# Two PSUM banks per GLA tile instead of four: values, keys and scores in one, output and state update in the other

## The chip, the cores and the metric

The kernel runs on one core of a Trainium2 chip. The metric is the time of one execution on the device, in microseconds (us); the median of three runs of the kernel before is 1786.33 us. All data is 32-bit floating point.

Engines: PE is the matrix engine, ACT the scalar engine, DVE the vector engine, POOL the general-purpose engine, and SP the engine that issues most transfers. PE writes its results to PSUM, of which this kernel uses eight banks of 512 fp32 numbers per partition; ACT and DVE read them from there.

## The reference

One decoder layer is computed for 2048 new tokens of one prompt and for 8 short continuations of 8 tokens each. The input x is projected by one wide matrix; the pieces feed sliding-window attention and a gated linear attention (GLA), both are gated, projected, merged, projected again, and a layer norm ends it. The change is in GLA, whose reference is a scan over chunks, with one state S per head:

```
b = jnp.cumsum(gc, axis=1); b_last = b[:, -1]
qt = qc * jnp.exp(b); kt = kc * jnp.exp(-b); kend = kc * jnp.exp(b_last[:, None] - b)
o_inter = jnp.einsum('bthk,bhkv->bthv', qt, S)
A = jnp.where(causal, jnp.einsum('bthk,bshk->bhts', qt, kt), 0.0)
o_intra = jnp.einsum('bhts,bshv->bthv', A, vc)
S = jnp.exp(b_last)[..., None] * S + jnp.einsum('bshk,bshv->bhkv', kend, vc)
```

There are 4 heads, keys of 128 and values of 256 numbers per head. The output o_inter + o_intra is divided by its root mean square and multiplied by a gate.

## The kernel before

**The projections** fill nearly all of PE's time. A product of fp32 numbers is made of three products of a reduced type: an operand is split into a high and a low part (`split`, lines 141 to 145: ACT casts the high part, line 142, then DVE or POOL subtracts it, line 143), and high x high, high x low and low x high are added up (lines 1335 to 1337). Large projections save one product in eight by a scheme with seven sums of blocks. There are four accumulator banks, pd0 to pd3, used in turn; ACT or DVE reads each out in `combine` and in the sinks (lines 199 to 229 and 384 to 410). The work is done in passes: x0, x1, x2 (input projections of three token ranges), then a0, u0, a1, u1, a2, u2 (the projections after attention and after GLA). Operands of a pass are loaded into tiles r (from xT, ua_d or ug_d) and split into tiles x.

**The side work.** Attention and GLA run as small pieces between the groups of the projections. Each piece has a due time in ticks of the projections' progress (`at`, `tick`, lines 124 to 130); `gla_phase` (line 1190) sets the times. PE's instructions stand in exactly the written order (`manual_schedule`, line 66). For the other engines the order is sorted when the kernel is built, by a scheduler that reckons with the waits between instructions; each engine then takes its own list strictly in order.

**GLA per tile of 128 tokens and head.** 64 such tiles are worked, in three phases; in the last phase each head ends with the continuations' tokens (`samp_a`, `samp_b`).

- `gla_v` (line 1071): PE transposes the values (two, line 1076) and the decayed keys (one, line 1077) into one bank; ACT and DVE split the 384 columns into gv and gl.
- `gla_a` (line 1087): PE makes the scores (line 1090) in a second bank; DVE copies them under the causal mask (line 1092) and ACT and POOL split them into ah.
- `gla_b` (line 1107), some one and two thirds of a tile's time later: PE reads the old state (line 1119) into the output's bank op, makes the state's update with three products into a fourth bank sp, and adds the three products of scores and values to op (all by the helper `three`, line 1113). DVE makes the new state from sp (line 1127; 1125 for a head's first tile). ACT squares and sums op (line 1101), POOL takes the power (lines 1102 and 1103), ACT scales op into on (line 1104).
- `gla_c` (line 1132), again as much later: PE transposes on into another bank (line 1136), and DVE multiplies it by the gate sg (line 1138). `gla_store` sends the result to ug_d, from where the passes u0 to u2 load it.

**The banks.** All side work takes its PSUM tiles from one pool of four banks (line 64), by `pa()`:

```
psa = ctx.enter_context(tc.tile_pool(name="psa", bufs=4, space=PSUM))
```

A request gets a bank that an earlier request had, and the first product into it waits until that tile's last reader is done. Which bank a request gets is fixed when the kernel is built. In the program before, the transposes of line 1136 mostly follow the state update of a later tile's `gla_b` (its reader is line 1127), the state's update follows a tile of scores (reader: line 1092), the output follows an earlier output (reader: line 1104), the scores follow an earlier line 1136 (reader: line 1138), and the values follow earlier values (readers: lines 142 and 143). The low-rank gate projection (`lowrank`, line 544) and attention take their tiles from the same pool.

Of the kernel before, what the change touches and what calls it, by code (L numbers as in the profile page):

```python
# [21 lines left out]
P = 128  # L22
# [15 lines left out]
HK = 128  # L38
HV = 256
# [18 lines left out]
def kernel(ctx, tc, io):  # L58
    nc = tc.nc
    mm = nc.tensor.matmul  # L60
# [15 lines left out]
    def pa():  # L76
        return psa.tile([P, 512], F32, tag="pa", name="pa")
# [18 lines left out]
    def mt(tag, n, bufs, dt=F32, name=None):  # L96
        return M["p"].tile([P, n], dt, tag=tag, name=name or tag, bufs=bufs)
# [43 lines left out]
    def split(dst_h, dst_l, src, eng=nc.vector):  # L141
        pin["a"] = nc.scalar.copy(dst_h, src)  # L142
        i = eng.tensor_tensor(dst_l, src, dst_h.bitcast(F32), ALU.subtract)  # L143
        if eng is nc.vector:
            pin["d"] = i
# [111 lines left out]
    for n, (kind, s, kh, prs) in enumerate(sets):  # L257
        start_of.append(len(groups))
        base.append(int(tk))
        for pr_ in prs:  # L260
# [5 lines left out]
            elif seq[n] in PLAIN:  # L266
                jk = [(j, k) for j in range(2) for k in range(2)]
                for c in range(2):
                    for j, k in jk if kind == "a" else [(j, k) for k, j in jk]:
                        q, p = pr_[j]  # L270
# [730 lines left out]
    def rot(key):  # L1001
        r = R[key][cnt[key] % len(R[key])]
        cnt[key] += 1
        return r
# [66 lines left out]
    def gla_v(B, i):  # L1071
        n = P if i < B["nt"] else NS
        ts = slice(i * P, i * P + n)
        tp = pa()
        for m in range(2):
            nc.tensor.transpose(tp[:n, m * P:(m + 1) * P], B["zvv"][:, m, ts], ident)
        nc.tensor.transpose(tp[:n, HV:HV + HK], B["k2"][:, ts], ident)
        if n == P:
            B["gv", i] = rot("gv"), rot("gl")
            split(*B["gv", i], tp[:, :HV + HK])  # L1080
            return
        g = mt("pr2", 2 * GU, 6, name="gs")[:, :HV + HK]
        nc.scalar.copy(g[:n], tp[:n, :HV + HK])
        nc.vector.tensor_copy(g[NS:], tp[:n, :HV + HK])
        B["gv", i] = g[:, :HV], g[:, HV:]

    def gla_a(B, i):
        ts = slice(i * P, (i + 1) * P)
        ap = pa()
        mm(ap[:, :P], B["k"][:, ts], B["q"][:, ts], start=True, stop=True)  # L1090
        A_ = rot("a")
        nc.vector.copy_predicated(A_, cmask.bitcast(U32), ap[:, :P])
        x = rot("ah")
        split(x[:, :P], x[:, P:], A_, nc.gpsimd)
        B["a", i] = x[:, :P], x[:, P:]

    def gla_norm(B, key, o, n):

        on = rot("on")
        sq = small([P, 1], "sq")  # L1100
        nc.scalar.activation(on[:n], o, AF.Square, scale=1.0 / 16, accum_out=sq[:n])
        nc.gpsimd.tensor_scalar(sq[:n], sq[:n], EPS, None, op0=ALU.add)
        nc.gpsimd.tensor_tensor(sq[:n], sq[:n], mhalf[:n], ALU.pow)
        nc.scalar.mul(on[:n], o, sq[:n])
        B["on", key] = on

    def gla_b(B, i):
        ts = slice(i * P, (i + 1) * P)
        gh, gl = B["gv", i]

        def three(ps, w, x, start):
            for j, (a, c) in enumerate(((w[0], x[0]), (w[1], x[0]), (w[0], x[1]))):
                mm(ps, a, c, start=start and j == 0, stop=(j == 2))  # L1113

        gv, kT2 = (gh[:, :HV], gl[:, :HV]), (gh[:, HV:], gl[:, HV:])
        S = sstate.get(B["h"])
        op = pa()
        if S is not None:
            mm(op[:, :HV], B["qb"][:, ts], S_t[S], start=True, stop=False)  # L1119
        sp = pa()  # L1120
        three(sp[:, :HV], kT2, gv, True)
        three(op[:, :HV], B["a", i], gv, S is None)
        Sn = S_free.popleft()
        if S is None:
            nc.vector.tensor_copy(S_t[Sn], sp[:, :HV])
        else:
            nc.vector.scalar_tensor_tensor(S_t[Sn], S_t[S], B["e1"][:, i:i + 1], sp[:, :HV], ALU.mult, ALU.add)
            S_free.append(S)
        sstate[B["h"]] = Sn
        gla_norm(B, i, op[:, :HV], P)  # L1130
# [59 lines left out]
    def gla_phase(s, t0, st):  # L1190
# [5 lines left out]
        for h, (c0, T_) in ([(h, c) for c in GCH[s] for h in range(GH)] if s == 1 else  # L1196
                            [(h, c) for h in range(GH) for c in GCH[s]]):
            if True:
# [10 lines left out]
                for i in range(nt):  # L1209
                    at(tt(u + i), lambda B=B, i=i: gla_v(B, i))  # L1210
                    at(tt(u + i), lambda B=B, i=i: gla_a(B, i))
                    at(tt(u + i + 5 / 3), lambda B=B, i=i: gla_b(B, i))
                    at(tt(u + i + 10 / 3), lambda B=B, i=i: gla_c(B, i, P, i * P))
# [3 lines left out]
                if last:  # L1217
                    u += 1
                    at(o - 5, lambda B=B: samp_state(B))
                    at(o, lambda B=B: gla_v(B, B["nt"]))  # L1220
                    at(o + 2, lambda B=B: samp_a(B))
                    at(tt(u - 1 + 0.5) + 2, lambda B=B: nc.sync.dma_start(io["o_sp"][B["h"]], S_t[sstate[B["h"]]]))
                    o = max(o + 6, tt(u - 1 + 4 / 3) + 1)
                    at(o, lambda B=B: samp_b(B, 0))
                    at(o + 2, lambda B=B: samp_b(B, 2))
                    at(o + 5, lambda B=B: gla_c(B, "s", NS, B["Tp"]))
                    at(max(o + 6, tt(u + 4 / 3) + 1), lambda B=B: gla_store(B))
                else:
                    at(tt(u + 7 / 3) + 1, lambda B=B: gla_store(B))
        return int(b0 + st * (nu + 7 / 3) + 3)  # L1230

    for s in range(MS):
        for t in range(2):
            B = dict(s=s, t=t)
# [73 lines left out]
    for g, (n, q, i, s, p, b, ch) in enumerate(groups):  # L1308
# [19 lines left out]
        ps = (banks[b] if b < 4 else banks2[b - 4])[:, :T]  # L1328
        if n == U2 and g >= start_of[U2] + 16:
            ps = banks2[b][:, :T]  # L1330
        for k in range(q.kh):
            ks, ts = slice(k * P, (k + 1) * P), slice(k * T, (k + 1) * T)
# [261 lines left out]
```

## Time and profile before

| | |
|---|---|
| median of three runs, without the profile | 1786.33 us (1783.8 to 1787.14) |
| the profiled execution's own time | 1796.17 us |
| its span, first to last instruction | 1794.4 us |
| granted clock of PE, mean over the span | 0.992 |
| DMA | 452.36 MB, mean 252 GB/s |

The profile is of one execution. A row of its list of groups gives line, engine, operation, what is written <- what is read, the count, the busy time and the mean duration in ns, and behind the second bar the idle time of the engine ahead of these instructions, with what ended it. A row of the waits gives who waited <- for whom, the sum in us, the number of waits and the longest. A row of the timeline gives the start and the duration in us, and in square brackets the idle time ahead of it. A row of the table by stretches gives the stretch, its length, the busy time (and the count) of PE, PE's weight loads, DVE, ACT and POOL, then the granted clock of PE as a share of the full one, the DMA engines' share, and GB/s. Buffer numbers are left out of names: pa is any tile of the pool of four banks, pd any of the four accumulators.

### The profile page before, as it was taken

Reading aid. Unit: us, or ns where it says so; the run is one execution under the profiler, and the core shown is the slowest. Engines: PE = TensorE matmul, PEld = TensorE weight load, DVE = VectorE, ACT = ScalarE, POOL = GpSimd, SP = SyncE. Lnnn points to the kernel's source line nnn. Section 1 sums busy time; section 2 is a strip of 40 time slices with the busy share of each in tenths; the row PEclk is TensorE's granted clock in tenths of the full one; section 3 lists DMA queues with packets and bytes.
Section 4 is the critical chain, followed back from the end, with each engine's and each line's share of the span. In section 5 each row is a group of like instructions: output and inputs, shape, how many; then the busy total and the mean of one; then the engine's idle time right before and its main releaser. Section 6 shows DMA issues by size and latency. Waiting matters only on the chain.

```text
span 1794.4 us, 31950 instructions
## 1 busy us (share of the span) xinstructions
PE 1755.9 (98%) x11154; PEld 1653.1 (92%) x11154; DVE 1102.7 (61%) x2178; ACT 866.6 (48%) x2084; POOL 375.3 (21%) x522
## 2 busy tenths in 40 slices
PE   8999999998999999999999999999999999999998
PEld 8899988998999999999999999999989989998887
DVE  6655679778555477548655447645856645536666
ACT  4565566566574465557466346645433432311100
POOL 5334624454111000013211100000122122121111
PEclk9999999999999999999999999999999999999999
DMA  6789977986978977886879788879889968965531
GB/s 215 252 306 333 327 236 241 312 290 215 308 260 284 304 252 236 282 288 208 281 251 313 228 289 275 267 241 336 282 230 250 298 178 224 320 155 189 168 108 53
DMA packets 290913, 452.36 MB, mean 252 GB/s; under 512 B 29213, under 2 KB 210133, under 8 KB 290736
## 3 DMA queue, kind: packets, MB, share of 16 engines
q1 hardware_dynamic: 262896, 415.04, 70.3%
q10 hardware_dynamic: 20464, 26.24, 4.1%
q0 software_dynamic: 7392, 9.04, 3.6%
q8 instruction: 88, 1.44, 0.3%
q14 instruction: 73, 0.60, 0.1%
HBM read 297.52 MB, written 153.57 MB: 251 GB/s over the span
## 4 chain that ended last, share of the span: by engine, by line
PE 78%; DMA 8%; DVE 5%; ACT 4%; issue 2%; POOL 2%; SPq 1%; DVEq 0%; ACTq 0%; POOLq 0%
PE pd L1335 18%; PE pd L1337 18%; PE pd L1336 18%; PE pd L1399 3%; PE pd L1400 3%; PE pd L1398 3%; PE pa L1113 2%; PE pa L832 1%; PE pa L818 1%; PE pa L786 1%; PE pa L1119 1%; DMA ug_d<-sg 1%; POOL ws L348 1%; DMA mg_d<-fin 1%; PE pa L1335 1%
## 5 line engine op out<-in xcount | busy, mean ns | idle before, releaser
L143 DVE TENSOR_TENSOR wp<-ws,wp 128x512 fp32r<-128x512 f32 (+1 forms) x396 | 276.5, 701 | 204.9 <-ACT wp L142 189.4
L142 ACT CAST wp<-ws 128x512 fp32r<-128x512 f32 (+1 forms) x396 | 234.1, 595 | 193.9 <-PE pd L1337 129.8
L348 POOL TENSOR_TENSOR ws<-ws 128x256 f32<-128x256 f32 x162 | 148.4, 943 | 166.5 <-DVE wp L143 100.9
L143 POOL TENSOR_TENSOR ah<-aper,ah 128x128 fp32r<-128x128 f32 x64 | 36.2, 566 | 399.5 <-ACT ah L142 399.5
L1399 PE MATMUL pd<-woh,x 128*128 128x512 f32 (+1 forms) x272 | 102.4, 377 | 0.0
L1400 PE MATMUL pd<-wol,x 128*128 128x512 f32 (+1 forms) x272 | 102.4, 377 | 0.0
L1398 PE MATMUL pd<-woh,x 128*128 128x512 f32 (+1 forms) x272 | 102.4, 377 | 0.0
L384 ACT COPY m<-pd 128x352 f32<-128x352 f32 x146 | 66.3, 454 | 70.5 <-PE pd L1337 64.8
L1335 PE MATMUL pd<-x3h,wp 128*128 128x352 f32 x292 | 97.3, 333 | 1.8 <-DMA wp<-wk_w_g 1.2
L1335 PE MATMUL pd<-x6h,wp 128*128 128x352 f32 x292 | 97.0, 332 | 2.0 <-ACT m L384 2.0
L1335 PE MATMUL pd<-x1h,wp 128*128 128x352 f32 x292 | 96.7, 331 | 2.2 <-DVE fin L405 2.1
L1335 PE MATMUL pd<-x7h,wp 128*128 128x352 f32 x292 | 97.7, 334 | 0.9 <-DVE fin L201 0.9
L1335 PE MATMUL pd<-x5h,wp 128*128 128x352 f32 x292 | 96.6, 331 | 0.0
L1335 PE MATMUL pd<-x2h,wp 128*128 128x352 f32 x292 | 96.3, 330 | 0.0
L1335 PE MATMUL pd<-x4h,wp 128*128 128x352 f32 x292 | 96.2, 330 | 0.0
L1337 PE MATMUL pd<-x1h,wp 128*128 128x352 f32 x292 | 94.0, 322 | 0.7 <-DVE wp L143 0.7
L1337 PE MATMUL pd<-x7h,wp 128*128 128x352 f32 x292 | 94.6, 324 | 0.0
L1337 PE MATMUL pd<-x3h,wp 128*128 128x352 f32 x292 | 94.5, 324 | 0.0
L1336 PE MATMUL pd<-x7l,wp 128*128 128x352 f32 x292 | 94.4, 323 | 0.0
L1336 PE MATMUL pd<-x3l,wp 128*128 128x352 f32 x292 | 94.3, 323 | 0.0
L1337 PE MATMUL pd<-x6h,wp 128*128 128x352 f32 x292 | 94.2, 323 | 0.0
L1336 PE MATMUL pd<-x6l,wp 128*128 128x352 f32 x292 | 94.0, 322 | 0.0
(462 smaller groups left out, 5475.2 us busy)
## 6 DMA issues: line engine op xcount, KB each, us to landing
wp<-wk_w_g SPq DMA_DIRECT2D x96, 512.0 KB
ws<-w_g SPq DMA_DIRECT2D x120, 256.0 KB
wk_w_g<-wp SPq DMA_DIRECT2D x48, 512.0 KB
wp<-wk_w_ra SPq DMA_DIRECT2D x32, 512.0 KB
wp<-wk_w_rg SPq DMA_DIRECT2D x32, 512.0 KB
ws<-w_at SPq DMA_DIRECT2D x53, 256.0 KB
wp<-wk_w_at SPq DMA_DIRECT2D x24, 512.0 KB
ws<-w_pg SPq DMA_DIRECT2D x48, 256.0 KB
```

The costliest lines, as they stand in the source:

```text
L142: pin["a"] = nc.scalar.copy(dst_h, src)
L143: i = eng.tensor_tensor(dst_l, src, dst_h.bitcast(F32), ALU.subtract)
L348: nc.gpsimd.tensor_tensor(o[:, c], x[:, c], y[:, c], op)
L384: nc.scalar.copy(A[i], ps)
L786: mm(ps[kv][:, j, k0:], A["q"][x][r, g0 + j, :], A["k"][y][r, k0:], start=(n == 0), stop=(n == 2), tile_position=(kv * HD, 0))
L1113: mm(ps, a, c, start=start and j == 0, stop=(j == 2))
L1335: mm(ps, wh, xh[:, ts], start=first, stop=False, skip_group_check=ch)
L1336: mm(ps, wh, xl[:, ts], start=False, stop=False, skip_group_check=ch)
L1337: mm(ps, wl, xh[:, ts], start=False, stop=(k == q.kh - 1 and not (type(i) is tuple and i[1] == 0)), skip_group_check=ch)
L1398: mm(ps, xh[:, xs], hi, start=(k == 0), stop=False)
L1399: mm(ps, xl[:, xs], hi, start=False, stop=False)
L1400: mm(ps, xh[:, xs], lo, start=False, stop=(k == KT - 1))
```

## The change

`gla_v` asks for a bank as before and now makes the scores too, in the columns behind values and keys (256 + 128 + 128 = 512). `gla_a` asks for none and reads the scores there. `gla_b` asks for one bank, whose first half is the output and whose second half is the state's update; the update's three products come first, then the read of the old state, then the three products of scores and values. A tile asks the pool three times instead of five. The arithmetic is the same.

```diff
@@ gla_v
-        tp = pa()
+        tp = B["va", i] = pa()
...
         nc.tensor.transpose(tp[:n, HV:HV + HK], B["k2"][:, ts], ident)
         if n == P:
+            mm(tp[:, HV + HK:], B["k"][:, ts], B["q"][:, ts], start=True, stop=True)
             B["gv", i] = rot("gv"), rot("gl")
@@ gla_a
-        ap = pa()
-        mm(ap[:, :P], B["k"][:, ts], B["q"][:, ts], start=True, stop=True)
+        ap = B["va", i][:, HV + HK:]
@@ gla_b
-        op = pa()
+        ps = pa()
+        op, sp = ps[:, :HV], ps[:, HV:]
+        three(sp[:, :HV], kT2, gv, True)
         if S is not None:
             mm(op[:, :HV], B["qb"][:, ts], S_t[S], start=True, stop=False)
-        sp = pa()
-        three(sp[:, :HV], kT2, gv, True)
         three(op[:, :HV], B["a", i], gv, S is None)
```

Lines 1090 and 1119 of the kernel before are lines 1079 and 1121 of the changed one; the other lines named here keep their numbers from line 1092 on, except 1119 and 1120.

What this makes of the lists of the engines is shown at three places. The first is PE's list at a `gla_b` between two products of the projections; gv and gl are the split values and keys, gb the query operand, S the old state, ah the split scores.

```order
 L1336 MATMUL pd_75<-x1l,wp 128x352
 L1337 MATMUL pd_75<-x1h,wp 128x352
-L1119 MATMUL pa<-S_219,gb 128x256
 L1113 MATMUL pa<-gv 128x256
 L1113 MATMUL pa<-gv,gl 128x256
 L1113 MATMUL pa<-gl,gv 128x256
+L1121 MATMUL pa<-S_219,gb 128x256
 L1113 MATMUL pa<-gv,ah 128x256 x2
 L1113 MATMUL pa<-gl,ah 128x256
```

The read of the old state moved behind the three products of the state's update; nothing else moved, and this is so in every tile with an old state. Elsewhere on PE, only the line number of the scores differs, and PE's list of the projections is the same.

The second place is while pass a1 runs (its sink is line 219) and the operand x(0, 1) of a later pass is made. On ACT, before:

```order
L142 CAST x(0, 0)_17890<-r_17783 128x352 x2
L142 CAST wp<-ws 128x256 x2
L142 CAST gv<-pa 128x384
L1051 ACTIVATE em<-dm 128x256
L1052 ACTIVATE ek<-ek 128x256
L142 CAST ah<-aper_209 128x128
L1053 ACTIVATE dm<-dm 128x256
L1054 ACTIVATE gb<-gb 128x256
L142 CAST x(0, 1)_17949<-r_17812 128x352
L142 CAST wp<-ws 128x256
```

and in the changed kernel:

```order
L142 CAST x(0, 0)_17765<-r_17660 128x352
L142 CAST wp<-ws 128x256
L142 CAST x(0, 1)_17823<-r_17688 128x352
L142 CAST gv<-pa 128x384
L1051 ACTIVATE em<-dm 128x256
L1052 ACTIVATE ek<-ek 128x256
L1053 ACTIVATE dm<-dm 128x256
L1054 ACTIVATE gb<-gb 128x256
L142 CAST ah<-aper_209 128x128
L142 CAST wp<-ws 128x256
```

The cast of x(0, 1), which needs a loaded tile r, moved ahead of the split of the values and of the decay factors. On DVE at the same place, before:

```order
L143 TENSOR_TENSOR gl<-pa,gv 128x384
L143 TENSOR_TENSOR wp<-ws,wp 128x256
L219 SCALAR_TENSOR_TENSOR fin<-part,pd_77 128x352
L1056 COPY e_17167<-gb 128x2
L1067 TENSOR_TENSOR em<-zkq,em 128x256
L219 SCALAR_TENSOR_TENSOR fin<-part,pd_74 128x352
L1138 TENSOR_TENSOR sg<-pa,sg 128x2x128
L143 TENSOR_TENSOR wp<-ws,wp 128x256
L1067 TENSOR_TENSOR ek<-zkq,ek 128x256
L1069 SCALAR_TENSOR_TENSOR dm<-zkq,dm 128x256
L1069 SCALAR_TENSOR_TENSOR gb<-zkq,gb 128x256
L143 TENSOR_TENSOR x(0, 1)_17949<-r_17812,x(0, 1)_17949 128x352
```

and in the changed kernel:

```order
L143 TENSOR_TENSOR wp<-ws,wp 128x256
L143 TENSOR_TENSOR x(0, 1)_17823<-r_17688,x(0, 1)_17823 128x352
L143 TENSOR_TENSOR gl<-pa,gv 128x384
L1092 COPY_PREDICATED aper_209<-cmask,pa 128x128
L219 SCALAR_TENSOR_TENSOR fin<-part,pd_77 128x352
L219 SCALAR_TENSOR_TENSOR fin<-part,pd_74 128x352
L1138 TENSOR_TENSOR sg<-pa,sg 128x2x128
```

The second half of the split of x(0, 1) now stands ahead of two read-outs of accumulators (L219), and the masked copy of the scores (L1092) behind the split of the values instead of ahead of it, as in every tile.

The third place is on ACT at the change from pass x2 to a0, where L1101 squares an output and L211 reads out an accumulator. Before:

```order
L142 CAST wp<-ws 128x256
L212 DMA rg_d<-fin 128x352
L1101 ACTIVATE on,sq<-pa 128x256
L142 CAST x(1, 1)h<-r_15531 128x704
L1104 ACTIVATE on<-pa,sq 128x256
L142 CAST x(1, 1)h<-r_15531 128x704
L211 ACTIVATE fin<-pd_74 128x352
```

and in the changed kernel:

```order
L142 CAST wp<-ws 128x256
L212 DMA rg_d<-fin 128x352
L142 CAST x(1, 1)h<-r_15434 128x704
L1101 ACTIVATE on,sq<-pa 128x256
L142 CAST x(1, 1)h<-r_15434 128x704
L1104 ACTIVATE on<-pa,sq 128x256
L211 ACTIVATE fin<-pd_74 128x352
```

L1101 moved behind a cast. In the built program it now also waits for the state update of its own tile on DVE (L1127), where it waited for PE; the casts of gv wait for the scores' product, where they waited for the last transpose.

## The prediction

> **What bounds the kernel now.** I read the page first, for the engine that has no room left.
>
> ```profile
> span 1794.4 us, 31950 instructions
> PE 1755.9 (98%) x11154; PEld 1653.1 (92%) x11154; DVE 1102.7 (61%) x2178; ACT 866.6 (48%) x2084; POOL 375.3 (21%) x522
> ```
>
> PE is busy for 98% of the span, and the change takes no product away. So it can give back only PE's waits: 1794.4 - 1755.9 = 38.5 us in all. The view of PE's waits says which of them are waits for a bank of the four-bank pool (those whose tile is pa):
>
> ```profile
> PE pa L1136 <- DVE S L1127: 4.0, 2, 3.7
> PE pa L1136 <- DVE S L1186: 3.6, 1, 3.6
> PE pa L544 <- DVE S L1127: 2.2, 1, 2.2
> ...
> PE pa L1113 <- DVE aper L1092: 1.3, 1, 1.3
> ```
>
> Five waits of the GLA part stand here, 4.0 + 3.6 + 2.2 + 1.3 = 11.1 us. In each of them a product needs a bank whose last reader, on DVE, is late. No row of that view has PE waiting for the split scores (POOL L143) or for the new state as an operand (L1119): the arithmetic chain of GLA has slack, the banks have not. The second cost of a wait is in the table by stretches. Here are three of the waits in the order of time, the stretches just behind them, and one that holds a shorter wait:
>
> ```profile
> 423.35 1.13 PE L544 MATMUL pa<-r,wg 128*32 128x352 f32 x12 [2.19 <-DVE S L1127]
> 1329.25 0.69 PE L1136 MATMUL pa<-ident,on 128*128 128x128 f32 x2 [3.74 <-DVE S L1127]
> 1449.14 0.69 PE L1136 MATMUL pa<-ident,on 128*128 128x128 f32 x2 [3.58 <-DVE S L1186]
> ...
> 424.20:427.70 3.50, 3.50 (x25) 1.20 (x18) 2.78 (x9) 2.72 (x9) 0.47 (x1) 0.51 0.57 154
> 1328.80:1332.30 3.50, 3.05 (x11) 3.05 (x12) 2.57 (x7) 0.69 (x2) 1.28 (x2) 0.51 0.93 305
> 1448.20:1455.20 7.00, 6.06 (x21) 5.38 (x22) 6.54 (x27) 2.42 (x7) 1.55 (x2) 0.51 0.98 313
> ...
> 200.00:250.00 50.00, 47.98 (x327) 45.95 (x327) 37.72 (x74) 31.20 (x85) 22.08 (x24) 1.00 0.79 274
> ```
>
> The granted clock (the third number from the end) is 0.51 behind the waits of 2.2, 3.7 and 3.6 us. That loses 3.5 x 0.49 = 1.7, again 1.7, and 7.0 x 0.49 = 3.4 us, 6.8 in all. With the waits themselves that is 17.9 us, the most that freeing banks can bring.
>
> **The change part by part.**
>
> *Two requests fewer per tile.* A tile asks the pool three times instead of five. In the built order the transposes of L1136 now get, in most tiles, a bank that held values, keys and scores, the output/state bank takes over from an earlier L1136, and the values from an earlier output/state bank. At all five waits above, the last reader of the new bank is an earlier instruction than the late one and stands, on its engine, ahead of the work that made that one late. So I take the five waits as gone. What is late next has to be read place by place: how much earlier may PE come before it meets the next accumulator (pd) that is not yet read out?
>
> ```profile
> 437.43 0.45 ACT L388 COPY u<-pd 128x352 f32<-128x352 f32 x1
> 440.79 0.32 PE L1335 MATMUL pd<-x5h,wp 128*128 128x352 f32 x1
> 1337.41 0.51 DVE L227 SCALAR_TENSOR_TENSOR fin<-part,pd 128x352 f32<-128x352 f32 x1
> 1340.28 0.32 PE L1335 MATMUL pd<-x(0, 1)h,wp 128*128 128x352 f32 x1
> 1462.21 0.51 DVE L227 SCALAR_TENSOR_TENSOR fin<-part,pd 128x352 f32<-128x352 f32 x1
> 1466.85 0.33 PE L1335 MATMUL pd<-x(0, 0)h,wp 128*128 128x352 f32 x1
> ```
>
> Each pair is a read-out and the first product that overwrites the same accumulator. Place A, 414 to 428 us: saved 1.3 + 2.2 + 1.7 = 5.2; the read-out ends at 437.88, 2.9 before PE, so 2.9 is kept and 2.3 given back. Place B, 1325 to 1332: saved 3.7 + 1.7 = 5.4; the read-out ends at 1337.92, 2.4 before PE; kept 2.4, given back 3.0. Place C, 1445 to 1455: saved 3.6 + 3.4 = 7.0; it ends at 1462.72, 4.1 before PE; kept 4.1, given back 2.9. The remaining 0.3 (the short one of the two waits in the first row) meets an accumulator at once and is given back. Kept: 2.9 + 2.4 + 4.1 = 9.4 us. The bounds are 17.9 (read-outs move forward with PE) and about 1 (below).
>
> *State product before the read of the old state.* Per tile the same eight rows are issued, in another order. Two prices could change:
>
> ```profile
> L1119 PE MATMUL pa<-S,gb 128*128 128x256 f32 x120 | 36.7, 387 | 0.0
> L1113 PE MATMUL pa<-gv 128*128 128x256 f32 x64 | 29.4, 460 | 1.3 <-DVE aper L1092 1.3
> ...
> L1113 PE MATMUL pa<-gv,gl 128*128 128x256 f32 x64 | 18.2, 284 | 0.0
> ```
>
> The product that comes behind L1119 takes 460 - 284 = 176 ns more than its like. In the new order L1119 still stands once per tile between two products of the other type, so some other product pays that, and I take 0. If the order made one such step more or less per tile, it would be 60 x 0.176 = 10.6 us either way; the count of steps excludes it. The state read comes three products later, 3 x 0.284 = 0.85 us at most, which is hidden, since PE never waits for it.
>
> *One bank, several readers.* In the built order, the casts of L142 now wait for the scores too, the masked copy L1092 stands behind the split of L143, and the square L1101 waits for the state update L1127 instead of for PE.
>
> ```profile
> L1127 DVE SCALAR_TENSOR_TENSOR S<-S,e,pa x60: 450/475/482, 382.7 to 1497.6; 128x256 f32<-128x256 f32 x60
> ACT on L1101 <- PE pa L1113: 35.2, 31, 3.3
> ```
>
> The first two cost under 1 us each in a chain for which PE never waits: 0. The third is an added wait on ACT. Queued behind it are the casts of weights, the read-outs of accumulators by ACT, and the casts of loaded operands. It lasts at least one L1127, 0.475 us, and up to what DVE has in hand. ACT is 48% busy, and it already stands idle for PE ahead of L1101 in 31 places, so nearly all of it is covered; at about 1256 us it is not:
>
> ```profile
> 1255.85 0.39 ACT L1101 ACTIVATE on<-pa 128x256 f32<-128x256 f32 x1
> 1256.53 0.46 DVE L1127 SCALAR_TENSOR_TENSOR S<-S,e,pa 128x256 f32<-128x256 f32 x1
> 1258.54 0.46 ACT L211 ACTIVATE fin<-pd 128x352 f32<-128x352 f32 x1
> 1259.05 0.43 PE L1335 MATMUL pd<-x(0, 1)_14958,wp 128*128 128x352 f32 x1
> ```
>
> L1101 would start after 1256.99, 1.1 us later, and the read-out L211 two places behind it releases the accumulator that PE takes at 1259.05 with 0.05 us to spare. Between 0 and 1.1; I take 0.8.
>
> The Trainium skill speaks against this part ("PSUM — Partial Sum Buffer", section "PSUM bank collisions raise a hardware error"): two engines may not touch one bank on the same partitions at once, not even disjoint columns and not even both reading. So by the page the two readers of the new output/state bank cannot run side by side as they did in two banks; no run here shows such a collision. What this would do if ACT's cover were gone is the last of the rivals.
>
> *The order of the other engines.* DVE, ACT and SP are re-sorted from the first GLA tile on. One place matters. Near 1404 us the cast of the operand x(0, 1), which waits for its load, now stands ahead of the cast of gv on ACT, and its second half ahead of two read-outs (L219) on DVE.
>
> ```profile
> 1396.34 0.47 ACT L142 CAST gv<-pa 128x384 fp32r<-128x384 f32 x1
> 1404.59 0.49 ACT L142 CAST x(0, 1)_17949<-r 128x352 fp32r<-128x352 f32 x1 [3.69 <-DMA r<-ua_d]
> 1399.54 0.30 DVE L1092 COPY_PREDICATED aper<-cmask,pa 128x128 f32<-128x128 uint32 x1
> 1399.74 0.55 DVE L143 TENSOR_TENSOR gl<-pa,gv 128x384 fp32r<-128x384 f32 x1
> 1400.54 0.52 DVE L219 SCALAR_TENSOR_TENSOR fin<-part,pd 128x352 f32<-128x352 f32 x1
> 1403.32 0.32 PE L1335 MATMUL pd<-x(0, 0)_16374,wp 128*128 128x352 f32 x1
> ```
>
> The load lands at 1404.59 and its place on SP is unchanged. Then gv is cast to about 1405.5, and DVE does gl 0.55, L1092 0.30 (0.2 of it not overlapped) and L219 0.52, to about 1406.8. PE wants that accumulator at 1403.32: a new wait of 3.5 us. After waits of 2.2 to 3.7 the clock fell three times; with the even chance of another 1.7 I take 3.5 + 0.8 = 4.3 (bounds 0, if the load comes earlier, and 5.2).
>
> A row on the clock, and the rule: in the stretch from 200 to 250 the clock stayed at 1.00, though it holds this wait:
>
> ```profile
> PE pd L1335 <- ACT m L384: 2.0, 1, 2.0
> ```
>
> The Trainium skill ("TensorE: Matmul & The Clock Gate", section "Why this matters for your kernels") says to keep gaps under about 3 us, or the clock halves. The waits of 3.6 and 3.7 agree; the one of 2.2 at 423 us was followed by 0.51 all the same. By the page's bound, place A would not have lost its 1.7, and 17.9 would be 16.2.
>
> **The sum.** 9.4 - 0.8 - 4.3 = 4.3 us less. The profiled execution took 1796.17 us, 1.8 more than its span; the median without the profile is 1786.33, 9.8 lower. I carry the difference over: 1786.3 - 4.3 = 1782.0. A measurement tells about 0.2%, 3.6 us.
>
> **Rivals.**
>
> *The waits go and nothing is given back.* For it: read-outs on ACT and DVE follow PE, so they may move forward too. Against it: at B and C those engines stand still until a load of r lands, whatever PE does. All 17.9: 1768.4.
>
> *DVE is the limit at A, so nothing is kept there.*
>
> ```profile
> 416.00:420.70 4.70, 4.70 (x34) 4.68 (x34) 4.70 (x11) 4.39 (x12) 0.46 (x1) 1.00 0.67 199
> ```
>
> DVE (the third busy time) has no gap in that stretch, and its work stays the same; PE would meet an accumulator instead of a bank. Then 4.3 - 2.9 = 1.4 us are left: 1784.9, no change that can be told.
>
> *Slower: the late loads decide, not the banks.* ACT and DVE take their work in order, and a cast that waits for a load holds every read-out behind it. If at B and C PE then stands before an accumulator as long as it stood before a bank, and the clock falls again, they keep nothing, A keeps its first 1.3, and the new wait at 1403 costs 3.5 + 1.7, with 0.8 for ACT: 1.3 - 5.2 - 0.8 = 4.7 us more, 1791.0. With k kept at B and C the sum is 4.7 - k us more, so it is told as slower from k below 1.1 on. For it: the casts of x there wait for loads. Against it: the room of 2.4 and 4.1 us read above.
>
> *Slower: every hold on ACT reaches PE.* L1101, and all that ACT has behind it, waits for a state update in each tile with an old state: 60 x 0.475 = 28.5 us, so 1786.3 - 9.4 + 28.5 = 1805.4 with the banks' gain. It is told as slower once 13.0 of the 28.5 reach PE. Against it: the 35.2 us in which ACT stood idle ahead of L1101 anyway. This is the case that the Trainium skill's rule on banks would bring about.
>
> That the change doesn't do what it says is excluded: the built order has three requests per tile and the new place of L1121.
>
> **How the numbers follow.** Forecast (some kept, one new wait) 0.38; all kept 0.10; no change 0.29; the late loads 0.18; the holds 0.05. So faster by over 0.2% is 0.48, within 0.2% is 0.29, slower by over 0.2% is 0.23. The time is the forecast's, 1782.0. The range reaches to the loads' case and 1 us on, for the 1.1 that a hold may cost, 1792; below, three quarters of the way to the first rival, 1772. Outside it lie the holds and parts of the first rival and of the loads' case.
>
> **What would show it.** Right: no PE wait for pa with L1127, L1186 or L1092 as releaser in GLA's part; shorter waits for pd behind places A, B and C; one new PE wait of about 3.5 us for pd with L219, near 1400; L1101 released by DVE L1127. Wrong: pa waits of several us that remain; L1121 or its neighbours dearer by a tenth of a us per tile; waits for pd as long as the pa waits were; many PE waits for ACT's read-outs.

## The result, and the profile after

| | median, us | lowest to highest, us | executions | ratio to before, 95% interval |
|---|---|---|---|---|
| before | 1786.33 | 1782.58 to 1792.36 | 5 | |
| changed | 1801.48 | 1794.84 to 1804.96 | 5 | 1.0077, 1.0055 to 1.0100 |
| changed, measured again | 1798.63 | 1797.46 to 1806.29 | 4 | 1.0079, 1.0054 to 1.0104 |

The changed kernel is slower by 0.8%, some 14 us. Its profiled execution hides this: it took 1796.18 us, as long as the profiled execution of before (1796.17). The former is among the quickest of its kernel, the latter lies above all five timed executions of its own. So the two pages can't be subtracted from each other; what happens in each can still be read. The head of the page of the changed kernel:

```profile
span 1794.1 us, 32013 instructions
PE 1755.8 (98%) x11154; PEld 1654.7 (92%) x11154; DVE 1100.7 (61%) x2178; ACT 865.3 (48%) x2084; POOL 368.7 (21%) x522
```

No engine is busier than before. PE's waits in the changed kernel, rows of GLA's part and behind it (L1186 is the state update of the continuations' tokens):

```profile
PE pd L1335 <- ACT fin L211: 3.4, 1, 3.4
PE pd L1335 <- ACT u L388: 2.8, 1, 2.8
PE pd L1335 <- DVE fin L393: 2.7, 1, 2.7
...
PE pd L1335 <- DVE fin L227: 1.1, 2, 0.7
PE pa L1136 <- DVE S L1186: 1.0, 1, 1.0
...
PE pa L1113 <- DVE S L1186: 0.4, 1, 0.4
```

The waits for a bank released by L1127 and L1092 are gone, and those by L1186 are 1.4 us in place of 3.6. The change did to the banks what it was built to do. In their place stand waits for accumulators (pd), and their releasers are ACT's read-outs L211 and L388 and a read-out of DVE. The view of ACT's waits shows what became of ACT; these are its three rows on GLA's normalisation and scores:

```profile
ACT on L1101 <- DVE S L1127: 78.6, 46, 3.9
ACT on L1104 <- POOL sq L1103: 71.4, 65, 3.4
ACT ah L142 <- DVE aper L1092: 33.5, 36, 2.4
```

Before, ACT stood ahead of L1101 for PE, 35.2 us in 31 waits. Now it stands there for DVE's state update, 78.6 us in 46 waits, 78.6 / 46 = 1.7 us each, though one L1127 takes 0.47. Most of the rest is what DVE has ahead of the update in its list: during the 78.6 us DVE is busy for 67.8, of which 21.4 are the updates themselves and 26.6 are splits (L143). The wait ahead of L1104 is little shorter than it was in the profile of before:

```profile
ACT on L1104 <- POOL sq L1103: 79.2, 63, 4.4
```

The timelines of DVE and ACT show one such place in the changed kernel (the last number is the idle time ahead of the instruction):

```profile
425.52 0.88 DVE L143 TENSOR_TENSOR x4l<-cx,x4h 128x704 fp32r<-128x704 f32 x1
426.33 0.47 DVE L1127 SCALAR_TENSOR_TENSOR S<-S,e,pa 128x256 f32<-128x256 f32 x1
424.85 1.14 ACT L142 CAST wp<-ws 128x512 fp32r<-128x512 f32 x2
426.83 0.39 ACT L1101 ACTIVATE on<-pa 128x256 f32<-128x256 f32 x1 [0.83 <-DVE S L1127]
429.20 0.48 ACT L1104 ACTIVATE on<-pa,sq 128x256 f32<-128x256 f32 x1 [1.89 <-POOL sq L1103]
429.57 0.45 ACT L384 COPY m<-pd 128x352 f32<-128x352 f32 x1
```

DVE splits an operand, then updates the state. ACT is done at 425.99 and waits for the update's end at 426.80. Only then can it square, only then can POOL take the power, and ACT waits for that too. Behind both stands L384, the read-out of an accumulator, which needed neither.

### The profile page after: what moved, and what is told of

It is laid out like the page before. It is cut to its first block, busy times and chain, and to the rows that moved or that the text cites. A ratio compares the mean times of both kernels' runs of the same rounds, so it can differ in the third digit from the quotient of the medians.

```text
span 1794.1 us, 32013 instructions
## 1 busy us (share of the span) xinstructions
PE 1755.8 (98%) x11154; PEld 1654.7 (92%) x11154; DVE 1100.7 (61%) x2178; ACT 865.3 (48%) x2084; POOL 368.7 (21%) x522
## 4 chain that ended last, share of the span: by engine, by line
PE 83%; DVE 5%; DMA 5%; ACT 3%; issue 2%; POOL 1%; SPq 0%; DVEq 0%; ACTq 0%; POOLq 0%
PE pd L1335 20%; PE pd L1337 19%; PE pd L1336 19%; PE pd L1399 3%; PE pd L1398 3%; PE pd L1400 3%; PE pa L1113 2%; PE pa L832 1%; DVE wp L143 1%; PE pa L818 1%; PE pa L786 1%; PE pa L1121 1%; DMA r<-ug_d 1%; DMA ws<-w_at 1%; PE pa L1076 1%
## 5 line engine op out<-in xcount | busy, mean ns | idle before, releaser
L143 DVE TENSOR_TENSOR wp<-ws,wp 128x512 fp32r<-128x512 f32 (+1 forms) x396 | 275.8, 699 | 237.8 <-ACT wp L142 223.0
L143 POOL TENSOR_TENSOR ah<-aper,ah 128x128 fp32r<-128x128 f32 x64 | 35.2, 550 | 436.0 <-ACT ah L142 436.0
L1335 PE MATMUL pd<-x2h,wp 128*128 128x352 f32 x292 | 97.2, 333 | 2.8 <-DVE fin L393 2.7
L1335 PE MATMUL pd<-x6h,wp 128*128 128x352 f32 x292 | 96.8, 332 | 1.3 <-ACT m L384 1.3
L384 ACT COPY m<-pd 128x352 f32<-128x352 f32 x146 | 66.1, 454 | 65.8 <-PE pd L1337 60.9
L1337 PE MATMUL pd<-x2h,wp 128*128 128x352 f32 x292 | 94.5, 324 | 0.0
L1336 PE MATMUL pd<-x2l,wp 128*128 128x352 f32 x292 | 94.3, 323 | 0.0
```

The lines of the kernel that those rows point to most:

```text
L384: nc.scalar.copy(A[i], ps)
L1335: mm(ps, wh, xh[:, ts], start=first, stop=False, skip_group_check=ch)
L1336: mm(ps, wh, xl[:, ts], start=False, stop=False, skip_group_check=ch)
L1337: mm(ps, wl, xh[:, ts], start=False, stop=(k == q.kh - 1 and not (type(i) is tuple and i[1] == 0)), skip_group_check=ch)
```

## The experiments

Ratios are to the kernel before on the same chip, with their 95% intervals.

**1. Values, keys and scores in one bank, nothing else.** `gla_v` and `gla_a` as changed, `gla_b` as before; the edit to the changed kernel:

```diff
-        ps = pa()
-        op, sp = ps[:, :HV], ps[:, HV:]
-        three(sp[:, :HV], kT2, gv, True)
+        op = pa()
         if S is not None:
             mm(op[:, :HV], B["qb"][:, ts], S_t[S], start=True, stop=False)
+        sp = pa()
+        three(sp[:, :HV], kT2, gv, True)
```

> Values, keys and scores share a bank as in the change; output and state update have a bank each, in the old order. The hold theory (what costs time is that ACT's square L1101 waits for DVE's state update L1127, 78.6 us in 46 waits in the changed kernel): that wait is gone here, so at most as slow as the kernel before, 1786 or less, and ACT waits ahead of L1101 for PE alone. The order theory (any re-sorting of ACT and DVE moves read-outs of accumulators behind late work): slower than before by some 5 to 15 us here too. The third theory (the scores' place delays the mask copy and the split scores): as slow as the changed kernel, about 1801.

Measured: 1787.73 us, 0.9998 (0.9983 to 1.0013). This half of the change costs nothing and brings nothing. ACT waits ahead of L1101 for PE again:

```profile
ACT on L1101 <- PE pa L1113: 24.0, 23, 3.3
```

**2. Output and state update in one bank, nothing else.** `gla_b` as changed, `gla_v` and `gla_a` as before.

> Output and state update share a bank, state product first, as in the change; values and scores have a bank each as before. The hold theory: L1101 waits for L1127 by 70 to 80 us in all and the time is that of the changed kernel, about 1801. The order theory: 5 to 15 us over before, with holds or without. The theory that the scores' place costs the time: as before, 1786.

Measured: 1797.75 us, 1.0056 (1.0038 to 1.0075). The cost lies in this half. ACT and PE wait so:

```profile
ACT on L1101 <- DVE S L1127: 84.2, 46, 4.3
...
PE pa L1113 <- ACT on L1104: 8.1, 3, 4.3
```

With the scores in banks of their own PE even waits for banks that ACT releases late.

**3. The order of PE alone.** The kernel before, with the three state products ahead of the read of the old state, every request its own bank:

```diff
-        op = pa()
+        op, sp = pa(), pa()
+        three(sp[:, :HV], kT2, gv, True)
         if S is not None:
             mm(op[:, :HV], B["qb"][:, ts], S_t[S], start=True, stop=False)
-        sp = pa()
-        three(sp[:, :HV], kT2, gv, True)
```

> Only the order in the output's step is changed, the three state products ahead of the read of the old state; every tile keeps its own bank. All theories on banks: as before, 1786, within 3. If the new order costs PE 0.176 us more per tile, 60 x 0.176 = 10.6 us more, 1797, and the groups L1113 and L1119 show it. ACT's order is nearly untouched and DVE's is moved in places, so the order theory allows some us either way.

Measured: 1790.48 us, 1.0015 (0.9999 to 1.0030): not told apart from before, and not the 1797 of a dearer order.

**4. The square written ahead of the state update.** The changed kernel, with the wait between the two readers of the shared bank turned round:

```diff
+        on, sq = rot("on"), small([P, 1], "sq")
+        nc.scalar.activation(on, op[:, :HV], AF.Square, scale=1.0 / 16, accum_out=sq)
         Sn = S_free.popleft()
...
-        gla_norm(B, i, op[:, :HV], P)
+        gla_norm(B, i, op[:, :HV], P, (on, sq))
```

> The changed kernel with the square of the output written ahead of the state update, so that DVE's update waits for ACT's square, and not the square for the update. Banks and PE's order are those of the change. The hold theory: ACT waits ahead of the square only for PE, some 35 us in all, and the time falls by 10 us or more from 1801, to 1782 to 1791, with the waits for banks still gone. The order theory: anywhere between 1782 and 1805, with waits at new places. If the hold costs nothing: 1801.

Measured: 1790.46 us, 1.0021 (1.0004 to 1.0039): of the change's 0.77% nearly three quarters are gone, 1.0077 / 1.0021 = 1.0056. The square is line 1123 here, the scaling 1103; ACT's waits:

```profile
ACT on L1103 <- POOL sq L1102: 68.6, 51, 4.5
...
ACT on L1123 <- PE pa L1112: 26.1, 26, 3.3
...
ACT on L1103 <- DVE S L1128: 16.4, 7, 3.7
```

A wait for the update is left ahead of the scaling, 16.4 us in seven places. POOL's power was done 0.4 to 2.6 us earlier there, so some 9 of the 16.4 us are the update's alone; the rest ACT would have waited for POOL.

**5. The wait alone.** The kernel before, all banks and PE's order untouched; ACT's square is made to wait for its tile's state update (the state update's two forms return `up`):

```diff
-        nc.scalar.activation(on[:n], o, AF.Square, scale=1.0 / 16, accum_out=sq[:n])
+        i2 = nc.scalar.activation(on[:n], o, AF.Square, scale=1.0 / 16, accum_out=sq[:n])
+        if up is not None:
+            tc.add_manual_dep(i2.ins, up.ins.name, mybir.DependencyInfo(mybir.DependencyClass.Sync, mybir.DependencyReason.DATA), reason="hold")
```

> The kernel before, banks and order of PE untouched, with one thing added: ACT's square L1101 has to wait for the state update L1127 (1125) of its own tile, as it does in the changed kernel. The hold theory: L1101 waits for DVE by 70 to 85 us in all, and the time rises by about what the change cost, 8 to 17 us, to 1795 to 1804. The rival, that what costs is the sharing itself (other banks for other tiles, other waits): no more than 3 us over before, 1790 or less.

Measured: 1796.09 us, 1.0049 (1.0030 to 1.0069). The wait came out a little shorter than expected:

```profile
ACT on L1101 <- DVE S L1129: 61.1, 42, 4.3
```

**6. The wait alone, with the lists of all other engines pinned.** As 5, and every instruction of ACT, DVE, POOL and SP tied behind the one that stands ahead of it in the kernel before:

```diff
+    for names in _ORDER.values():
+        for a, b in zip(names, names[1:]):
+            tc.add_manual_dep(made[f"I-{b}"], f"I-{a}", info, reason="order of before")
```

> The kernel before with the square's wait for the state update added, as in the run with the hold alone, and with the lists of ACT, DVE, POOL and SP pinned to those of the kernel before, instruction by instruction: nothing but the wait differs. If the wait itself costs the time: 1.003 to 1.007 times the kernel before, 1791 to 1798, as with the hold alone (1.0049). If the cost came from the few places at which the wait made the lists be sorted otherwise (56 of ACT's, 19 of DVE's, 10 of POOL's and 18 of SP's): within 0.15% of the kernel before.

Measured: 1793.54 us, 1.0057 (1.0035 to 1.0079). In the traces ACT, DVE and POOL run their instructions in the order of before without an exception, the banks and PE's order are those of before too; only the wait was added, and it costs what it cost in 5. So the cost isn't that of a re-sorted list. ACT's rows (L1129 is the state update here, L1127 that of a head's first tile):

```profile
ACT on L1101 <- DVE S L1129: 65.9, 45, 3.5
...
ACT on L1101 <- DVE S L1127: 4.7, 3, 3.7
```

**7. The kernel before once more, for its trace.**

> The kernel before once more, for a second trace. If the waits for banks of 3.7 and 3.6 us and the clock's falls behind them belonged to the one profiled execution of 1796.17, which is 9 us over the median: this one, near 1787, shows them short or not at all, and no half clock behind 1300 us. If they are in every execution: again some 11 us of waits for banks in GLA's part and 6.8 us of lost clock.

Measured: 1783.73 us (one execution), with a span of 1781.9. PE's waits for banks in GLA's part:

```profile
PE pa L1113 <- DVE aper L1092: 1.9, 1, 1.9
...
PE pa L1136 <- DVE S L1127: 1.8, 2, 1.2
PE pa L1136 <- DVE S L1186: 1.3, 1, 1.3
...
PE pa L544 <- DVE S L1127: 0.6, 1, 0.6
```

And its table by stretches, all that lies behind 1300 us and the one stretch of half clock near GLA's waits:

```profile
1300.00:1770.00 470.00, 466.39 (x2701) 425.88 (x2700) 274.96 (x567) 119.75 (x278) 94.13 (x127) 1.00 0.71 206
415.30:418.80 3.50, 3.50 (x14) 3.50 (x15) 3.50 (x8) 3.19 (x10) 0.46 (x1) 0.53 0.50 140
```

The same waits as in the first profile of before, but 5.6 us in place of 11.1, and one stretch of half clock in GLA's part in place of three: 3.5 x 0.47 = 1.6 us in place of 6.8. What freeing banks could bring in this execution was 7.2 us, not 17.9.

**8. The changed kernel once more.**

> The changed kernel once more. The first measurement gave 1801.48 and a profiled execution of 1796.18. Expected: 1797 to 1804 and again 70 to 85 us of waits of L1101 for L1127; if its profile is of a slower execution than the first, it shows more waits for accumulators released by ACT (L388, L211) and more half clock.

Measured: 1798.63 us, 1.0079; the profiled execution took 1799.43. Its L1101 waits 79.3 us for L1127.

**9. Square first, and the scaling three ticks later.**

```diff
+                    at(tt(u + i + 5 / 3) + 3, later(lambda B=B, i=i: B["scale", i]()))
                     at(tt(u + i + 10 / 3), lambda B=B, i=i: gla_c(B, i, P, i * P))
```

> As with the square written first, and ACT's scaling L1104 written three ticks later, so that fewer instructions of ACT stand behind its wait for POOL's power (71 to 87 us in all so far). A generalised hold theory (any wait at the head of ACT's list is paid partly by PE): the wait falls to under 55 us and the time to 1780 to 1787, below the 1790.5 with the square first. If only the hold by the state update mattered: 1788 to 1792. If the longer stay in the bank decides: waits of PE for pa released by the scaling, and 1792 or more.

Measured: 1784.86 us, 0.9997 (0.9982 to 1.0012). ACT's waits ahead of the scaling (lines 1107 and 1105 here) fell from 68.6 + 16.4 us to 42.2:

```profile
ACT on L1107 <- POOL sq L1102: 27.9, 20, 4.5
ACT on L1107 <- DVE S L1131: 10.0, 4, 3.1
...
ACT on L1105 <- POOL sq L1102: 4.3, 4, 1.3
```

**10. The late scaling in the kernel before.**

> The kernel before, with ACT's scaling L1104 written three ticks later; five requests of banks per tile as before. If waits at the head of ACT's list are what PE pays for: L1104's wait for POOL falls from about 84 us to under 50, and the time to 1778 to 1784. If the longer stay of the output in its bank costs as much, since this kernel has no banks to spare: PE waits for pa released by the scaling, and 1786 or more. Against the square first with the late scale (1784.9) it also tells what two requests fewer are worth.

Measured: 1789.55 us, 1.0021 (1.0003 to 1.0039): a miss for the theory that every wait of ACT is paid by PE. ACT's wait for POOL fell from 79.2 to 35.3 us and nothing was won. PE's waits for pa don't name the scaling as releaser either, so the other expectation isn't shown.

**11. The late scaling with values and scores in one bank (1 and 9 together).**

> Values, keys and scores in one bank, output and state update apart, and the late scale: four requests per tile, no wait of the square for the state update. The hold theory: the best of all, 1778 to 1785, with L1104's wait under 50 us. If the shared bank of values and scores has a price that was hidden in its run alone (1787.7): 1786 or more.

Measured: 1784.97 us, 1.0002 (0.9986 to 1.0018): no better than 1 alone.

**12. The late scaling in the changed kernel.**

> The changed kernel with the late scale alone: the square still waits for the state update. The hold theory: the 78.6 us of waits of L1101 stay, those of L1104 fall, and some 4 to 7 us of 1801 are won, 1793 to 1797, still over the kernel before. If the late scale alone undoes the change's cost: 1785 to 1788.

Measured: 1794.54 us, 1.0050 (1.0031 to 1.0069). Both of ACT's waits, in one view:

```profile
ACT on L1101 <- DVE S L1130: 80.8, 45, 3.8
ACT on L1108 <- POOL sq L1103: 32.6, 28, 4.3
```

The wait for POOL fell to less than half, the wait for the update stayed, and the kernel is still slower than before. Against 9, which differs from it only in which of the two readers goes first: 1.0050 / 0.9997 = 1.0053.

**What follows from all of them.** The wait of L1101 for L1127 costs 0.49% (5), 0.57% (6), 0.56% (changed against 4) and 0.53% (12 against 9) of 1786 us: 9 to 10 us, four times by different ways, each known to about 0.2%. That this part is the wait's, and neither the sharing's nor the re-sorting's, is shown. Nor is it the sum of ACT's idle time that PE pays for: ahead of square and scaling together ACT waits 80.8 + 32.6 = 113.4 us in run 12, no more than in the first trace of before (35.2 + 79.2 = 114.4), and run 12 is 0.5% slower all the same. The remaining 0.2% of the change is the distance of 4 to before, 1.0021, in which new places in the lists, what the banks bring and the wait of 16.4 us are together; these runs don't split it. No kernel tried is clearly quicker than before; the version of 9 keeps the three requests per tile and is level with it.

Where the time goes is seen when the start of the same product of PE is compared in two traces. The differences to the second trace of before, in us, by stretches of that trace:

| stretch, us | before, first trace | changed | changed again | wait alone, lists pinned (6) | square first, late scaling (9) |
|---|---|---|---|---|---|
| to 371 (ahead of GLA's banks) | 2.2 | 3.6 | 1.1 | 1.4 | 1.0 |
| to 429 | 0.0 | -2.3 | -2.1 | -1.1 | -6.8 |
| to 475 | 0.0 | 4.2 | 6.8 | 0.3 | 2.1 |
| to 898 | 0.0 | 3.4 | 2.3 | 2.3 | 1.1 |
| to 1233 | 0.8 | 0.6 | 1.0 | -0.7 | -0.6 |
| to 1265 | -1.6 | 3.2 | 3.5 | -0.3 | -1.0 |
| to 1359 | 3.9 | -0.5 | -0.4 | 3.9 | -0.5 |
| to 1421 | 0.5 | -0.2 | 3.4 | 1.5 | 2.3 |
| to 1484 | 4.2 | -0.6 | -0.8 | 2.0 | -0.5 |
| to the end | 2.3 | 0.9 | 0.6 | 0.9 | 1.3 |
| sum | 12.4 | 12.1 | 15.4 | 10.3 | -1.6 |

Up to 429 us the changed kernel makes up 2 us, and with ACT freed (9) 6.8. The 2 us aren't clear of what one trace can tell: run 3, with its five requests per tile, makes up 2.7 there, and run 6 makes up 1.1. The changed kernel gives them back by 475 with 2 to 5 us on top. Giving back alone isn't the work of the wait either: runs 1 and 4, in which the square doesn't wait for the update, make up 4.2 and 5.7 by 429 and give back 4.2 and 5.2. From one trace of each, a single row of this table also holds what differs from execution to execution: before has 3.9 and 4.2 in the two rows of places B and C in one execution, none in the other. And run 6 loses its 10.3 us elsewhere than the changed kernel, 5.9 of them in those two rows. So the time that the wait costs is shown by the runs; the way from the wait to PE, place by place, is not.

## Why the prediction was wrong

The forecast was 1782.0 with a range to 1792; the kernel stands at 1801, so the sign was wrong too.

**The step that failed: "One bank, several readers".** It named the new wait of L1101 for L1127, its length ("up to what DVE has in hand"), and what is queued behind it, rightly. It then took "nearly all of it" as covered, because ACT is busy 48% and already stood idle ahead of L1101 in 31 places, and put 0.8 us for one place. Measured: 9 to 10 us. The two arguments fail for these reasons. The idle time ahead of L1101 was short of the new wait: 35.2 us against 78.6 (the step never summed the wait; the rival took 0.475 per tile, and it is 1.7 per wait). And idle time of ACT is not spare time at the places that count: POOL's power starts only when the square is done, so L1104's wait follows later and hardly shrinks (79.2 and 84.0 us in the two traces of before, 71.4 and 70.8 in those of the changed kernel), and read-outs and casts are behind both. DVE in turn waits for ACT's casts. This row of DVE's waits is of the changed kernel, where the two traces of before have 200.2 and 204.2:

```profile
DVE wp L143 <- ACT wp L142: 233.8, 171, 6.4
```

The rival "every hold on ACT reaches PE" had the mechanism and a chance of 0.05. Its price of 28.5 us was three times too high: the waits came to 78.6 us, and an eighth of them reaches PE. That its 1805.4 lies nearest to the result is in part luck, since it also took off 9.4 us that did not come. The Trainium skill's rule that it rested on ("PSUM — Partial Sum Buffer", section "PSUM bank collisions raise a hardware error"), that two engines may not read one bank on the same partitions at once, is obeyed here by a wait, and the trace agrees with the order it forces: L1127 ends at 426.80, L1101 starts at 426.83, and in both traces of the changed kernel all 64 squares start behind their tile's update, while in the first trace of before 54 of the 64 start ahead of its end.

**The second failure: "Kept: 9.4 us", and "I carry the difference over".** The waits at B and C and the half clock behind them, 3.7 + 3.6 + 1.7 + 3.4 = 12.4 us, stood in an execution that took 9.8 us more than the median. The second trace of before, at 1783.73, has 1.2 + 1.3 and no half clock there. As far as two traces tell, most of the waits to be saved were thus the excess of that one execution, and taking the saving off the median took off what the median had not. Such waits come and go: run 10, at 1787.01 in its trace, has one of 3.2 us at B with half clock behind it. The sum needs to be made against an execution near the median, or the excess of the profiled one taken out first.

**Place A**: right that waits for accumulators would take the place of the bank waits, wrong why. "The read-out ends at 437.88" was taken as fixed, with PE coming earlier. PE came no earlier to this product (440.90 against 440.79 us in the first traces, 438.54 against 438.51 in the second ones); the read-out L388 came later, at 443.66, and PE waited 2.8 us. Right ahead of it ACT stood 1.8 us for POOL at L1104. The wait of 2.7 us for L393 is at 408 us, ahead of place A. "Kept 2.9" did not come about: by 475 us the changed kernel is 2 to 5 us behind. The rival "DVE is the limit at A" had the outcome; the releaser is ACT.

**Places B and C**: right that the waits by L1127 go and that short ones follow: 0.4 us for L227 at B in each trace. By L1186 1.4 and 1.1 us were left at C. What was saved there is 0.4 to 0.5 and 0.6 to 0.8 us against the second trace of before (the rows to 1359 and 1484), no more than other rows differ by.

**The reordering at 0**: right. The 176 ns moved from one product to another, and the sum stayed. A group of the kernel before, and then three of the changed kernel:

```profile
L1113 PE MATMUL pa<-gv,ah 128*128 128x256 f32 x128 | 25.7, 282 | 0.0
...
L1113 PE MATMUL pa<-gv,ah 128*128 128x256 f32 x128 | 36.8, 368 | 0.0
L1121 PE MATMUL pa<-S,gb 128*128 128x256 f32 x120 | 35.8, 379 | 0.0
...
L1113 PE MATMUL pa<-gv 128*128 128x256 f32 x64 | 18.4, 287 | 0.4 <-DVE S L1186 0.4
```

The first product by gv went from 460 to 287, -173 ns; the two by ah went from 282 to 368 on the mean, 2 x 86 = +172.

**The new wait near 1403, 4.3 us**: half right. ACT does stand there for the load of x(0, 1), 5.0 us in the first trace of the changed kernel and 7.0 in the second:

```profile
1407.89 0.49 ACT L142 CAST x(0, 1)_17823<-r 128x352 fp32r<-128x352 f32 x1 [4.96 <-DMA r<-ua_d]
```

```profile
1410.04 0.48 ACT L142 CAST x(0, 1)_17823<-r 128x352 fp32r<-128x352 f32 x1 [7.01 <-DMA r<-ua_d]
```

PE's wait behind it, in the waits of the second trace:

```profile
PE pd L1335 <- ACT ah L142: 2.0, 1, 2.0
```

PE pays nothing for it in the first and 2.0 us with a fall of the clock, 3.4 in all, in the second. Whether it is paid depends on when the load lands; the bounds 0 to 5.2 hold.

**"At about 1256 us" 0.8**: 3.4 us of waiting for L211 in both traces, and half clock behind; the second trace of before waits 1.6 there as well. ACT at this place in the changed kernel:

```profile
1264.72 0.78 ACT L142 CAST x(1, 1)h<-r 128x704 fp32r<-128x704 f32 x1 [1.64 <-DMA r<-ug_d]
1265.41 0.38 ACT L1101 ACTIVATE on<-pa 128x256 f32<-128x256 f32 x1
1267.93 0.47 ACT L1104 ACTIVATE on<-pa,sq 128x256 f32<-128x256 f32 x1 [1.39 <-POOL sq L1103]
1268.30 0.46 ACT L211 ACTIVATE fin<-pd 128x352 f32<-128x352 f32 x1
```

L1101 does not wait for the update here. It is late because in the new list it stands behind a cast that waits for its load, and then L1104 waits for POOL ahead of L211. Where the scaling comes later (12) PE waits 0.85 us for L211. So the step had the right read-out and the wrong wait: what is lost here comes from the new place in the list.

## What to carry to other kernels

Before two tiles share a bank, see what their readers then wait for. Values and scores, read by ACT and DVE one after the other, shared theirs at no cost (1). Output and state update made a reader that had been free wait for the other one's whole queue; with the order of the two turned round most of the cost was gone (4). Before counting a new wait as covered by idle time, ask whether that idle time stands at the same place, how long the releaser's list ahead is, and what else starts only after the waiting instruction. A saving read from one profiled execution that is 10 us over its kernel's median is first of all a reading of that excess: compare with a second trace before taking it off.

## What the runs showed of the hardware

**The same wait does and does not cost the clock.** In both traces of the changed kernel PE waits 2.82 us for L388 at the same product. The first is followed by full clock, the second by half clock for 7 us. The product in the timelines of the first and of the second:

```profile
443.72 0.43 PE L1335 MATMUL pd<-x5h,wp 128*128 128x352 f32 x1 [2.82 <-ACT u L388]
```

```profile
441.36 0.66 PE L1335 MATMUL pd<-x5h,wp 128*128 128x352 f32 x1 [2.82 <-ACT u L388]
```

The stretch behind it in the tables by stretches, of the first and of the second:

```profile
443.60:447.10 3.50, 3.38 (x22) 3.33 (x23) 2.88 (x6) 1.69 (x5) 2.48 (x3) 1.00 0.44 143
```

```profile
440.60:447.60 7.00, 6.24 (x23) 6.07 (x24) 5.61 (x12) 3.56 (x8) 3.57 (x5) 0.52 0.77 249
```

That is 7.0 x 0.48 = 3.4 us between two executions of one program, by nothing that differs in the length of the wait; what decides it these traces don't tell. The Trainium skill ("TensorE: Matmul & The Clock Gate", section "Why this matters for your kernels") asks for gaps under about 3 us; both gaps are under it, and one was halved all the same.

**Waits and clock make up the difference between executions of one kernel, but not between kernels.** Adding the rows of PE's waits, and (1 - mean clock) x span: first trace of before 29.7 + 0.008 x 1794.4 = 44.1 us at 1796.17; second 24.3 + 0.004 x 1781.9 = 31.4 at 1783.73; changed 29.7 + 0.006 x 1794.1 = 40.5 at 1796.18; changed again 28.9 + 0.008 x 1797.3 = 43.3 at 1799.43; the version of 9, 21.1 + 0.003 x 1780.3 = 26.4 at 1782.12. What remains is 1752.1 and 1752.3 for the two of before, 1755.7 and 1756.1 for the two of the changed kernel, and 1755.7 for run 9. So of the 15.7 us between the second traces of before and of the changed kernel 11.9 are waits and clock, and 3.8 are in neither. In all fourteen traces the remainder lies between 1750 and 1758: for two executions of one kernel it served as a yardstick here, for two kernels it is uncertain by as much as half of what this change costs.
